# Loading the first units of a grouped normalization in row halves over two DMA queues

## The chip, the cores and the metric

The kernel runs on one core of a Trainium2 chip. The metric is the device time of one execution in microseconds (us), as the median of several runs. A core has five engines: TensorE (PE in the profile), VectorE (DVE), ScalarE (ACT), GpSimd (POOL) and SyncE (SP). The transfers between the chip's memory (HBM) and the on-chip memory (SBUF) are issued from the instruction streams of SyncE and ScalarE here, and 16 DMA engines carry them out.

## The reference

The input is x with the shape (4, 8, 16, 256, 256) and gamma with (8, 16), both in float32. Every one of the 4 x 8 x 16 = 512 channels is normalized over its own 65,536 values and multiplied by its gamma:

```python
mu = x.mean(axis=(3, 4), keepdims=True)
var = ((x - mu) ** 2).mean(axis=(3, 4), keepdims=True)
x_norm = (x - mu) / np.sqrt(var + 1e-5)
out = x_norm * gamma[None, :, :, None, None]
```

So 134.22 MB are read and as much is written, and each value is needed twice: for the sums of its channel and for its own result.

## The kernel before, in words

The work is cut into 32 units of 16 channels. A unit is a tile of 128 partitions with 8,192 values each (4 MiB); eight partitions hold one channel, and one partition's row is 32 KB, contiguous in HBM. Six tiles, `slots` (`xt` in the profile), live in SBUF for the whole kernel; unit `u` uses slot `u % AHEAD`, with `AHEAD = 6`. A unit's result is written into its own slot, in place.

Nothing is reordered by a scheduler: each engine runs its instructions in the order of the program (`manual_schedule`), and waits are put in where data or slots require it. The tool that builds the program also gives each DMA one of eight semaphores in turn, so a DMA waits for the earlier one that used the same semaphore.

For each unit the loop does the following.

- VectorE sums each row (L103) while ScalarE sums the squares of each row (L104); both go to `st`.
- TensorE multiplies `st` with a constant matrix `navg`, which adds up the eight rows of a channel and gives each row the negative mean and the negative mean of squares (L112, into `ps`).
- VectorE forms the negative variance (L113), ScalarE the square root (L117), VectorE the reciprocal and the product with gamma (L121, L123), and then the whole tile is shifted and scaled in place (L126).
- ScalarE issues the store of the tile (L130). SyncE issues the load of unit `u + 6` into the same slot (the helper `load`, L48), once that store has landed.

Before the loop, the first six loads are issued without any wait, through the helper `load`. Units 0, 2, 4 and 5 go to SyncE's queue; gamma (`g_row`, L54) and units 1 and 3 go to ScalarE's. In the profile q1 is SyncE's queue and q10 ScalarE's. All later loads go to SyncE's queue, all stores to ScalarE's, each queue in order. Store 0 therefore stands behind units 1 and 3 in ScalarE's queue.

Of the kernel before, what the change touches and what calls it, by code (L numbers as in the profile page):

```python
# [1 line left out]

# [4 lines left out]

F32 = mybir.dt.float32
U8 = mybir.dt.uint8
ALU = mybir.AluOpType  # L10
ACTF = mybir.ActivationFunctionType
AX = mybir.AxisListType


@with_exitstack
def kernel(
    ctx: ExitStack,
    tc: tile.TileContext,
    x: bass.AP,
    gamma: bass.AP,  # L20
    out: bass.AP,
):
    nc = tc.nc
    B, G, C, H, W = x.shape
    P = nc.NUM_PARTITIONS
    HW = H * W
    n_ch = B * G * C
    S = 8
    K = P // S
    F = HW // S  # L30
    U = n_ch // K
    NG = (G * C) // K
    AHEAD = 6
    assert HW % S == 0 and (G * C) % K == 0

    xv = x.rearrange("b g c h w -> (b g c h w)").rearrange("(u p f) -> u p f", p=P, f=F)
    ov = out.rearrange("b g c h w -> (b g c h w)").rearrange("(u p f) -> u p f", p=P, f=F)
    gv = gamma.rearrange("g c -> (g c)")

    data = ctx.enter_context(tc.tile_pool(name="data", bufs=1))  # L40
    singles = ctx.enter_context(tc.tile_pool(name="singles", bufs=1))
    psum = ctx.enter_context(tc.tile_pool(name="psum", bufs=4, space=bass.MemoryType.PSUM))
    ctx.enter_context(tc.manual_schedule())

    slots = [data.tile([P, F], F32, name=f"xt{i}") for i in range(AHEAD)]

    def load(u, queue):
        queue.dma_start(out=slots[u % AHEAD][:], in_=xv[u])  # L48


    g_row = singles.tile([1, G * C], F32, name="g_row")
    for u in range(AHEAD):
        if u == 1:
            nc.scalar.dma_start(out=g_row[:], in_=gv[None, :])  # L54
        load(u, nc.scalar if u in (1, 3) else nc.sync)


    eps_t = singles.tile([P, 1], F32, name="eps_t")
    nc.gpsimd.memset(eps_t[:], 1e-5)
    one = singles.tile([1, 1], F32, name="one")  # L60
    nc.gpsimd.memset(one[:], 1.0)
    navg = singles.tile([P, K, S], F32, name="navg")
    nc.gpsimd.memset(navg[:], -1.0 / HW)  # L63
    nc.gpsimd.affine_select(  # L64
        out=navg[:], in_=navg[:], pattern=[[-S, K], [0, S]], compare_op=ALU.is_ge,
        fill=0.0, base=0, channel_multiplier=1,
    )
    nc.gpsimd.affine_select(  # L68
        out=navg[:], in_=navg[:], pattern=[[S, K], [0, S]], compare_op=ALU.is_ge,
        fill=0.0, base=S - 1, channel_multiplier=-1,  # L70
    )
    navg_w = navg[:].rearrange("p k s -> p (k s)")
    root_eps = singles.tile([P, 1], F32, name="root_eps")
    nc.scalar.activation(out=root_eps[:], in_=eps_t[:], func=ACTF.Sqrt)  # L74
    g_rep = singles.tile([1, NG, K, S], F32, name="g_rep")
    g_ps = psum.tile([P, NG], F32, name="g_ps", bufs=1)
    g_col = singles.tile([P, NG], F32, name="g_col")

    nc.vector.tensor_copy(  # L79
        out=g_rep[:],  # L80
        in_=g_row[:].rearrange("o (n k) -> o n k", n=NG).unsqueeze(3).to_broadcast([1, NG, K, S]),
    )
    for n in range(NG):
        nc.tensor.matmul(  # L84
            out=g_ps[:, n : n + 1],
            lhsT=g_rep[:, n].rearrange("o k s -> o (k s)"),
            rhs=one[:],
            start=True, stop=True,
        )
    nc.vector.tensor_copy(out=g_col[:], in_=g_ps[:])  # L90

    junk = singles.tile([P, F], U8, name="junk")

    st = singles.tile([P, U, 2], F32, name="st")
    nvar = singles.tile([P, U], F32, name="nvar")
    std = singles.tile([P, U], F32, name="std")
    rstd = singles.tile([P, U], F32, name="rstd")
    scale = singles.tile([P, U], F32, name="scale")

    squares = []  # L100
    for u in range(U):
        t = slots[u % AHEAD]
        nc.vector.reduce_sum(out=st[:, u, 0:1], in_=t[:], axis=AX.X)  # L103
        square = nc.scalar.activation(  # L104
            out=junk[:], in_=t[:], func=ACTF.Square, accum_out=st[:, u, 1:2],
        )
        if u:

            tc.declare_no_dep(square.ins, squares[-1].ins, reason="junk, ordered by the root between")
        squares.append(square)  # L110
        ps = psum.tile([P, 2], F32, name="ps")
        nc.tensor.matmul(out=ps[:], lhsT=navg_w, rhs=st[:, u], start=True, stop=True)  # L112
        nc.vector.tensor_scalar(  # L113
            out=nvar[:, u : u + 1], in0=ps[:, 0:1], scalar1=ps[:, 0:1],
            scalar2=ps[:, 1:2], op0=ALU.mult, op1=ALU.add,
        )
        nc.scalar.activation(  # L117
            out=std[:, u : u + 1], in_=nvar[:, u : u + 1], func=ACTF.Sqrt,
            bias=eps_t[:], scale=-1.0,
        )  # L120
        nc.vector.reciprocal(out=rstd[:, u : u + 1], in_=std[:, u : u + 1])  # L121
        g = u % NG
        nc.vector.tensor_mul(  # L123
            out=scale[:, u : u + 1], in0=rstd[:, u : u + 1], in1=g_col[:, g : g + 1],
        )
        nc.vector.tensor_scalar(  # L126
            out=t[:], in0=t[:], scalar1=ps[:, 0:1], scalar2=scale[:, u : u + 1],
            op0=ALU.add, op1=ALU.mult,
        )
        nc.scalar.dma_start(out=ov[u], in_=t[:])  # L130
        if u + AHEAD < U:
            load(u + AHEAD, nc.sync)


# [1 line left out]
_INS = ['x', 'gamma']  # L136
_OUTS = [((4, 8, 16, 256, 256), 'float32')]


# [23 lines left out]
```

## Time and profile before

| What | Value |
|---|---|
| median of 3 runs | 626.75 us (626.74 to 627.11) |
| the profiled execution's own time | 626.89 us |
| its span in the profile | 625.2 us |
| moved by DMA | 268.46 MB, mean 429 GB/s over the span |
| busy: VectorE, ScalarE, TensorE | 443.2 us, 238.8 us, 21.4 us |
| unit 0: sums begin, store issued | 20.32 us, 35.38 us |

The span runs from the first to the last recorded event of the profiled execution; the 1.7 us between it and the execution's own time lie around it. The profile cuts the span into 40 slices, each 15.6 us long, and gives a digit for each engine and for the DMA engines: 9 means busy for 90% or more. A line of a group names the source line, the engine, the operation, what it writes and reads, how often, the busy time and the mean duration. "To landing" is the time from the issue of a DMA to its completion. A DMA's packet is here one row of 32 KB, moved by one of the 16 DMA engines.

### The profile page before, as it was taken

To read this page: it belongs to the slowest core of one execution; us is meant where nothing else is said; L and a number is where in the kernel's file an instruction comes from. 1 tells how busy PE (TensorE), PEld (TensorE's weight loads), DVE (VectorE), ACT (ScalarE), POOL (GpSimd) and SP (SyncE) were. 2 spreads that over 40 slices of the span, in tenths; PEclk is the share of its full clock that TensorE was granted. 3 is DMA by queue.
4 is the path that set the end of the run, shared out by engine and by line. 5 is a ranking of instruction groups with operands and counts; after the bars stand their busy time and mean duration, and the time that the engine had idled before them with its cause. 6 is when DMAs were issued, how large, how long until landed. Compare 5 with 4: busy or idle time off the path is not lost.

```text
span 625.2 us, 626 instructions
## 1 busy us (share of the span) xinstructions
PE 21.4 (3%) x80; PEld 19.5 (3%) x80; DVE 443.2 (71%) x162; ACT 238.8 (38%) x98; POOL 1.3 (0%) x9
## 2 busy tenths in 40 slices
PE   2000000000000000000000000000000000000000
PEld 2000000000000000000000000000000000000000
DVE  0699999998867668676687766776667867668620
ACT  0444444444444224443244432344423443224400
POOL 0000000000000000000000000000000000000000
DMA  8999999999999999999999999999999999999998
GB/s 369 436 417 424 434 436 436 436 436 437 434 436 434 426 426 430 434 436 436 436 434 434 436 434 434 430 426 430 434 436 436 436 432 434 436 436 434 426 426 365
DMA packets 9220, 268.46 MB, mean 429 GB/s; under 512 B 1025, under 2 KB 1026, under 8 KB 1026
## 3 DMA queue, kind: packets, MB, share of 16 engines
q10 hardware_dynamic: 4898, 142.61, 52.8%
q1 hardware_dynamic: 4320, 125.83, 46.8%
q14 instruction: 2, 0.02, 0.0%
HBM read 134.22 MB, written 134.22 MB: 429 GB/s over the span
## 4 chain that ended last, share of the span: by engine, by line
another core or an unknown queue 64%; DMA 16%; DVE 13%; SPq 1%; PE 1%; issue 0%; ACT 0%
DMA xt<-in_x_dram 9%; DVE st L103 8%; DMA out_dram<-xt 7%; DVE xt L126 4%; SPq L48 1%; PE ps L112 1%; ACT std L117 0%; DVE nvar L113 0%; DVE rstd L121 0%; DVE scale L123 0%
## 5 line engine op out<-in xcount | busy, mean ns | idle before, releaser
L103 DVE TENSOR_REDUCE st<-xt 128x1 f32<-128x8192 f32 x32 | 277.9, 8684 | 111.2 <-DMA xt<-in_x_dram 111.2
L104 ACT ACTIVATE junk<-xt 128x8192 uint8<-128x8192 f32 x32 | 225.0, 7030 | 272.2 <-DMA xt<-in_x_dram 229.0
L126 DVE TENSOR_SCALAR xt<-xt,ps,scale 128x8192 f32<-128x8192 f32 x32 | 145.6, 4550 | 1.2
L117 ACT ACTIVATE std<-nvar,eps_t 128x1 f32<-128x1 f32 x32 | 9.4, 294 | 79.6 <-DVE nvar L113 79.6
L112 PE MATMUL ps<-st,navg 128*128 128x2 f32 x64 | 17.9, 349 | 568.0 <-DVE st L103 568.0
L112 PEld LDWEIGHTS ps<-st,navg 128*128 128x128 f32 x64 | 16.0, 312 | 569.8 <-issue 569.8
L113 DVE TENSOR_SCALAR nvar<-ps 128x1 f32<-128x1 f32 x32 | 9.2, 287 | 23.8 <-PE ps L112 23.8
L121 DVE RECIPROCAL rstd<-std 128x1 f32<-128x1 f32 x32 | 5.3, 164 | 11.6 <-ACT std L117 11.6
L104 ACT ACTIVATION_READ_ACCUMULATOR junk<-xt 128x1 f32 x32 | 6.0, 186 | 0.0
L123 DVE TENSOR_TENSOR scale<-rstd,g_col 128x1 f32<-128x1 f32 x32 | 5.1, 159 | 1.1
L84 PE MATMUL g_ps<-one,g_rep 1*128 1x1 f32 x16 | 3.5, 346 | 2.9 <-DVE g_rep L79 2.9
L84 PEld LDWEIGHTS g_ps<-one,g_rep 1*128 1x128 f32 x16 | 3.5, 325 | 2.9 <-POOL navg L68 2.9
L90 DVE COPY g_col<-g_ps 128x8 f32<-128x8 f32 x1 | 0.2, 166 | 3.7 <-PE g_ps L84 3.7
L74 ACT ACT_TABLE_LOAD x1 | 1.3, 1283 | 2.2 <-issue 2.2
L79 DVE COPY g_rep<-g_row 1x1024 f32<-1x1024 f32 x1 | 0.7, 681 | 2.1 <-DMA g_row<-in_gamma_dram 2.1
L64 POOL TENSOR_SCALAR_AFFINE_SELECT navg<-navg 128x128 f32<-128x128 f32 x1 | 0.4, 403 | 0.1
L68 POOL TENSOR_SCALAR_AFFINE_SELECT navg<-navg 128x128 f32<-128x128 f32 x1 | 0.4, 398 | 0.1
L63 POOL MEMSET navg<- 128x128 f32 x1 | 0.2, 220 | 0.0
L74 ACT ACTIVATE root_eps<-eps_t 128x1 f32<-128x1 f32 x1 | 0.2, 203 | 0.0
L147 POOL MEMSET const-bfloat16-1.0<- 128x1 bf16 x1 | 0.1, 101 | 0.0
L147 POOL MEMSET const-uint8-127<- 128x1 uint8 x1 | 0.1, 101 | 0.0
L147 POOL MEMSET const-float32-0.0<- 128x1 f32 x1 | 0.1, 98 | 0.3 <-issue 0.3
(3 smaller groups left out, 0.3 us busy)
## 6 DMA issues: line engine op xcount, KB each, us to landing
out_dram<-xt ACTq DMA_DIRECT2D x32, 4096.0 KB, 67.1
xt<-in_x_dram SPq DMA_DIRECT2D x30, 4096.0 KB, 33.8
xt<-in_x_dram ACTq DMA_DIRECT2D x2, 4096.0 KB, 33.3
g_row<-in_gamma_dram ACTq DMA_DIRECT2D x1, 0.5 KB
```

What stands on the lines that cost most here:

```text
L48: queue.dma_start(out=slots[u % AHEAD][:], in_=xv[u])
L74: nc.scalar.activation(out=root_eps[:], in_=eps_t[:], func=ACTF.Sqrt)
L79: nc.vector.tensor_copy(out=g_rep[:], in_=g_row[:].rearrange("o (n k) -> o n k", n=NG).unsqueeze(3).to_broadcast([1, NG, K, S]),)
L84: nc.tensor.matmul(out=g_ps[:, n : n + 1], lhsT=g_rep[:, n].rearrange("o k s -> o (k s)"), rhs=one[:], start=True, stop=True,)
L103: nc.vector.reduce_sum(out=st[:, u, 0:1], in_=t[:], axis=AX.X)
L104: square = nc.scalar.activation(out=junk[:], in_=t[:], func=ACTF.Square, accum_out=st[:, u, 1:2],)
L112: nc.tensor.matmul(out=ps[:], lhsT=navg_w, rhs=st[:, u], start=True, stop=True)
L113: nc.vector.tensor_scalar(out=nvar[:, u : u + 1], in0=ps[:, 0:1], scalar1=ps[:, 0:1], scalar2=ps[:, 1:2], op0=ALU.mult, op1=ALU.add,)
L117: nc.scalar.activation(out=std[:, u : u + 1], in_=nvar[:, u : u + 1], func=ACTF.Sqrt, bias=eps_t[:], scale=-1.0,)
L121: nc.vector.reciprocal(out=rstd[:, u : u + 1], in_=std[:, u : u + 1])
L123: nc.vector.tensor_mul(out=scale[:, u : u + 1], in0=rstd[:, u : u + 1], in1=g_col[:, g : g + 1],)
L126: nc.vector.tensor_scalar(out=t[:], in0=t[:], scalar1=ps[:, 0:1], scalar2=scale[:, u : u + 1], op0=ALU.add, op1=ALU.mult,)
```

## The change

Only the first six loads are altered. The helper `load` gets a range of partitions. Units 0 and 2 are each loaded by two DMAs: partitions 0 to 63 from SyncE's queue, partitions 64 to 127 from ScalarE's. Unit 1 stays whole on ScalarE's queue, unit 3 moves to SyncE's. ScalarE's queue now carries gamma, the upper half of unit 0, unit 1 and the upper half of unit 2, and then store 0; SyncE's carries the lower halves of units 0 and 2 and then units 3, 4 and 5. The loop is the same, and its lines stand four lines further down (L103 becomes L107, L130 becomes L134).

```diff
-    def load(u, queue):
-        queue.dma_start(out=slots[u % AHEAD][:], in_=xv[u])
+    def load(u, queue, lo=0, hi=P):
+        queue.dma_start(out=slots[u % AHEAD][lo:hi], in_=xv[u, lo:hi])
 
 
     g_row = singles.tile([1, G * C], F32, name="g_row")
-    for u in range(AHEAD):
-        if u == 1:
-            nc.scalar.dma_start(out=g_row[:], in_=gv[None, :])
-        load(u, nc.scalar if u in (1, 3) else nc.sync)
+    load(0, nc.sync, 0, P // 2)
+    nc.scalar.dma_start(out=g_row[:], in_=gv[None, :])
+    load(0, nc.scalar, P // 2, P)
+    load(2, nc.sync, 0, P // 2)
+    load(1, nc.scalar)
+    load(2, nc.scalar, P // 2, P)
+    for u in range(3, AHEAD):
+        load(u, nc.sync)
```

## The prediction, made before the run

> **What bounds the kernel now.** I read the page first, its slices and queues before its engine rows.
>
> ```profile
> PE 21.4 (3%) x80; PEld 19.5 (3%) x80; DVE 443.2 (71%) x162; ACT 238.8 (38%) x98; POOL 1.3 (0%) x9
> ...
> DMA  8999999999999999999999999999999999999998
> GB/s 369 436 417 424 434 436 436 436 436 437 434 436 434 426 426 430 434 436 436 436 434 434 436 434 434 430 426 430 434 436 436 436 432 434 436 436 434 426 426 365
> DMA packets 9220, 268.46 MB, mean 429 GB/s; under 512 B 1025, under 2 KB 1026, under 8 KB 1026
> ...
> q10 hardware_dynamic: 4898, 142.61, 52.8%
> q1 hardware_dynamic: 4320, 125.83, 46.8%
> ```
>
> No compute engine is full. The DMA row is at 9 in every slice but the first and the last: the 16 DMA engines have work all the time. [...] Then stretches of the span, first the steady middle, then the drain of stores, then the last microseconds:
>
> ```profile
> 60.00:580.00 520.00, 15.62 (x56) 14.04 (x56) 392.03 (x143) 207.91 (x85) 0.00 (x0) 1.00 1.00 434
> 580.00:622.00 42.00, 0.56 (x2) 0.50 (x2) 13.85 (x5) 7.42 (x3) 0.00 (x0) 1.00 1.01 435
> 622.00:625.20 3.20, 0.00 (x0) 0.00 (x0) 0.00 (x0) 0.00 (x0) 0.00 (x0) 1.00 0.07 31
> ```
>
> The last two columns are DMA share and GB/s. 268.46 MB at 434 GB/s is 618.6 us of the 625.2 us; nearly all the rest is the start (nothing moves before 1.8 us) and the tail. The drain, with stores alone in one queue, runs at 435: a single queue fills the engines. So the order of the transfers is worth nothing by itself, and **any time in which the DMA engines move less is added to the end in full**.
>
> The packet records of the trace give the unit. A row of a tile is one 32 KB packet; there are 8,192, so 512 for each engine, and the median one takes 1.213 us (27.0 GB/s). 512 x 1.213 = 621.1 us: back to back from 1.8 us to the drain's end. Each engine's first packet takes about 2.0 us (0.8 extra). The first three packets of each engine are q1's; only then, at 6.13 us, does q10 get its first row, and from there the queues take turns packet by packet.
>
> Last, the waits and the first unit:
>
> ```profile
> SPq L48 <- DMA out_dram<-xt: 536.6, 26, 61.7
> ```
> ```profile
> 20.32 8.69 DVE L103 TENSOR_REDUCE st<-xt 128x1 f32<-128x8192 f32 x1 [13.70 <-DMA xt<-in_x_dram]
> ...
> 35.38 0.35 ACTq L130 DMA_DIRECT2D out_dram<-xt  x1
> ```
>
> From the landing of unit 0 to the issue of store 0 is 35.38 - 20.32 = 15.06 us. SyncE waits for stores, yet its queue never runs dry: a load takes 33.8 us to land by the page's issue rows, against 19.4 us for one tile at half the bandwidth (4.19 MB / 217 GB/s). A store takes 67.1 us, so some three others stand before it. VectorE starting earlier or later is absorbed there.
>
> [...]
>
> **The change part by part.**
>
> *Two more DMA issues.* ScalarE's queue issues three x loads ahead of its table load instead of two, SyncE five in place of four. An issue costs 0.37 to 0.53 us. On ScalarE the table load moves from 2.24 to about 2.7 us, beside a wait for data that ends at 20.32 us: nothing. On SyncE all are issued by about 3 us, with tens of microseconds of data in front: nothing. If that cover were gone, 0.5 us each.
>
> *New waits.* In the changed instruction order, load 5 waits for g_row's semaphore, which it reuses; g_row had landed when g_rep began at 2.06 us, before SyncE gets there. Behind load 5 only load 6 is queued, which waits for store 0. Store 1 waits for the lower half of unit 2; behind it on ScalarE stands the square of unit 2. That half lands before 36 us in any case below, store 1 is ready at 45 or later: nothing. The sums of unit 0 wait for two halves.
>
> *Order and amounts.* ScalarE's queue still carries two units of loads ahead of store 0 (0.5 + 1 + 0.5 for 1 and 3), SyncE's four. So store 0 gets its turn after the same bytes, SyncE has about a unit left when store 0 lands, and neither queue runs dry. If DVE gets unit 0 early, nothing is gained: store 0 stands behind unit 1 and the half of unit 2 anyway.
>
> *The halves.* Each engine now moves 4 x 4 = 16 rows in half tiles (both halves of units 0 and 2). [...] If both of a pair are in the same half together, a packet takes up to 2 x 1.213 us. How exactly do they keep step? The sixteen engines' second packets start between 3.71 and 4.23 us; two taken at random are some 0.2 us apart. [...] So 16 x (1.213 - 0.2) = **+16.2 us**. Ends: d = 0 gives 16 x 1.213 = +19.4; d = 0.52, the whole spread, gives 16 x 0.69 = +11.1. Below nothing isn't excluded by a rule, but only the slow first packets (0.8 us) are there to be won.
>
> The lost time lies wholly on the bound resource, so the sum is 626.89 + 16.2 = 643.1 for the profiled execution; the median stands 0.14 us under it: 643.0.
>
> **The rivals.**
>
> *Pairs out of step.* One engine of a pair is in a lower half while the other is in an upper one; then both go at full rate in units 0 and lower 2. Lost remain the three packets before q10's first row, 3 x 1.0, and the upper half of unit 2, which alternates with whole rows from SyncE's queue: [...] 4 x 1.213 = 4.9. Sum +7.9: 634.7, with its spread 634 to 638. For it: queues alternate halves. Against: all engines start together.
>
> *Not slower: ports don't bind.* The engine's own rate, [...] is the 27.0 GB/s, or the halves go each to engines of their own. Then a half row takes 1.21 us, all packets still follow each other, and the 32 extra completion records cost too little to see: 626.8. It decides when the mean extra of a half row is under 1.25 / 16 = 0.08 us. For it: nothing in this trace shows a slow row after the first. [...]
>
> *Faster through an earlier first unit.* Unit 0 would be the tenth packet of each engine, 1.81 + 0.8 + 10 x 1.213 = 14.7 us, some 5 us early. That would count if VectorE set the end; it has 71% and the stores queue 67 us. Worth at most the 0.8 us: 626.0, inside the 0.2%.
>
> **How the numbers follow.** 0.2% is 1.25 us, about what a measurement of this kernel can tell from no change. In step 0.54, out of step or between 0.21, ports don't bind 0.23, a gain beyond 0.2% 0.02. So slower 0.75, same 0.23, faster 0.02. The likeliest gives 643.0, its own range is 637.9 to 646.2. Both slower cases hold 0.75, so the range has to reach down into the third: 626.6 to 646.5.
>
> **What would show it.** Right: packets of half rows near 2.2 us; the first two slices of GB/s well under 300 (a packet of 2.2 us on 16 engines is 238 GB/s) and another dip near 50 to 60 us, where the upper half of unit 2 alternates with whole rows (two packets in 3.4 us, about 310 GB/s); from then on 434 as before; unit 0's sum starts near 1.81 + 0.8 + 10 x 2.2 = 25 us, later than before, not earlier. Loads still 33.8 us to landing. Wrong: unit 0's sum at 15 us with 430 GB/s in slices 1 to 3 (ports don't bind), or slices after the fifth that fall below 426 (a queue that runs dry, which I excluded).

## The result, and the profile after

The changed kernel takes 647.32 us (median of 4 runs, 647.11 to 647.74) against 626.87 us before in the same comparison: a ratio of 1.0327 (95% interval 1.0309 to 1.0345), or 20.45 us more. The forecast was 643.0 us, slower, with a range up to 646.5: the direction and the place of the loss held, the size lies above the range. The 16.2 us in the forecast rest on an estimate of the author's that no trace of before shows: a half row takes up to twice the measured 1.213 us, less a lag d that stays the same from row to row. Three of the experiments below (e6_lag, e9_middle and e10_contig16) spread by more than 1.5% among their own runs; of those I use single times and stretches of the profile, and no ratio.

The page of the changed kernel, the rows that answer to those shown of before:

```profile
PE 21.4 (3%) x80; PEld 19.5 (3%) x80; DVE 443.4 (69%) x162; ACT 238.8 (37%) x98; POOL 1.3 (0%) x9
...
DMA  9999999999999999999999999999999999999998
GB/s 195 227 420 264 448 426 424 450 424 428 445 424 432 443 424 434 440 424 434 442 422 436 440 422 438 438 422 442 434 422 448 428 422 448 428 426 444 426 432 351
DMA packets 9252, 268.46 MB, mean 416 GB/s; under 512 B 1057, under 2 KB 1058, under 8 KB 1058
...
q10 hardware_dynamic: 4914, 142.61, 52.7%
q1 hardware_dynamic: 4336, 125.83, 46.8%
```

Bytes and the busy time of the engines are the same; 32 small packets more come with the two more DMAs (1,057 under 512 B against 1,025). The DMA row is even fuller than before, at 9 from the first slice on. Busy hides the loss: it is in the row below. Slices 1, 2 and 4 move 195, 227 and 264 GB/s, and from slice 5 on the row looks like that of before. In slices 1 and 2 the DMA engines were occupied and moved half of before's 369 and 436 GB/s.

The same stretches of both kernels show it without the averaging of the slices. The last two columns are DMA share and GB/s. First before, then the changed kernel:

```profile
3.00:26.00 23.00, 3.42 (x16) 3.33 (x16) 5.84 (x2) 6.40 (x3) 0.00 (x0) 1.00 1.00 432
26.00:36.00 10.00, 0.56 (x2) 0.50 (x2) 8.82 (x6) 1.96 (x4) 0.00 (x0) 1.00 0.98 423
36.00:50.00 14.00, 0.56 (x2) 0.50 (x2) 12.82 (x5) 7.19 (x3) 0.00 (x0) 1.00 1.00 412
50.00:65.00 15.00, 0.56 (x2) 0.50 (x2) 13.82 (x6) 7.42 (x3) 0.00 (x0) 1.00 0.99 428
65.00:600.00 535.00, 16.18 (x58) 14.54 (x58) 401.21 (x146) 215.09 (x87) 0.00 (x0) 1.00 1.00 433
```
```profile
3.00:26.00 23.00, 3.42 (x16) 3.33 (x16) 0.17 (x1) 1.49 (x2) 0.00 (x0) 1.00 0.96 207
26.00:36.00 10.00, 0.00 (x0) 0.00 (x0) 7.91 (x1) 7.12 (x2) 0.00 (x0) 1.00 1.01 285
36.00:50.00 14.00, 0.56 (x2) 0.50 (x2) 5.93 (x5) 0.29 (x1) 0.00 (x0) 1.00 1.00 431
50.00:65.00 15.00, 0.56 (x2) 0.50 (x2) 13.60 (x5) 7.42 (x3) 0.00 (x0) 1.00 1.02 275
65.00:600.00 535.00, 16.18 (x58) 14.53 (x58) 401.29 (x146) 215.08 (x87) 0.00 (x0) 1.00 1.00 433
```

Until about 34 us the halves of unit 0 and the lower half of unit 2 are in flight, from 50 to 65 us the upper half of unit 2; between them unit 1 and the whole rows of unit 3 go at full speed. Time lost, as the bytes missing at before's rate: 23 x (432 - 207) / 432 = 11.98, 10 x (423 - 285) / 423 = 3.26 and 15 x (428 - 275) / 428 = 5.36 us, together 20.6 us. Between 36 and 50 us the changed kernel wins back 14 x (431 - 412) / 412 = 0.6 us. That leaves 20.0 of the 20.8 us by which the spans differ (646.0 - 625.2). From 65 to 600 us both run at 433 GB/s: nothing is lost there and nothing won back.

The trace also has a record of each packet, with its start and its duration but without its engine. Following each packet to the one that starts where it ends gives 16 chains of some 512 rows each, one for each DMA engine. What is said below of the rows of an engine is read from these chains.

The first unit and SyncE's waits, the changed kernel:

```profile
28.09 8.69 DVE L107 TENSOR_REDUCE st<-xt 128x1 f32<-128x8192 f32 x1 [21.46 <-DMA xt<-in_x_dram]
...
43.14 0.36 ACTq L134 DMA_DIRECT2D out_dram<-xt  x1
```
```profile
SPq L48 <- DMA out_dram<-xt: 556.0, 26, 80.9
```

Unit 0, split over two queues, begins its sums at 28.09 us; whole, on one queue, it had begun at 20.32. From there to store 0 it takes 15.05 us as before. SyncE's longest wait, load 6 for store 0, grows from 61.7 to 80.9 us, but loads still take 33.8 us to land and stores 67.1, both as before: the queues behind are as full as they were.

### The profile page after: what moved, and what is told of

Same layout as the page of the kernel before. It is cut to its first block, busy times and chain, and to the rows that moved or that the text cites. A ratio compares the mean times of both kernels' runs of the same rounds, so it can differ in the third digit from the quotient of the medians.

```text
span 646.0 us, 633 instructions
## 1 busy us (share of the span) xinstructions
PE 21.4 (3%) x80; PEld 19.5 (3%) x80; DVE 443.4 (69%) x162; ACT 238.8 (37%) x98; POOL 1.3 (0%) x9
## 2 busy tenths in 40 slices
DMA packets 9252, 268.46 MB, mean 416 GB/s; under 512 B 1057, under 2 KB 1058, under 8 KB 1058
## 4 chain that ended last, share of the span: by engine, by line
another core or an unknown queue 65%; DMA 20%; DVE 9%; SPq 1%; PE 0%; issue 0%; ACT 0%; ACTq 0%; DVEq 0%
DMA xt<-in_x_dram 13%; DMA out_dram<-xt 7%; DVE st L107 5%; DVE xt L130 3%; SPq L48 1%; PE ps L116 0%; ACT std L121 0%; DVE nvar L117 0%; DVE rstd L125 0%; DVE scale L127 0%; ACTq L48 0%; ACTq L53 0%; DVEq L107 0%
## 5 line engine op out<-in xcount | busy, mean ns | idle before, releaser
L107 DVE TENSOR_REDUCE st<-xt 128x1 f32<-128x8192 f32 x32 | 277.9, 8685 | 131.8 <-DMA xt<-in_x_dram 131.8
L130 DVE TENSOR_SCALAR xt<-xt,ps,scale 128x8192 f32<-128x8192 f32 x32 | 145.6, 4550 | 1.2
## 6 DMA issues: line engine op xcount, KB each, us to landing
out_dram<-xt ACTq DMA_DIRECT2D x32, 4096.0 KB, 67.1
xt<-in_x_dram SPq DMA_DIRECT2D x29, 4096.0 KB, 33.8
```

The source lines that it names most:

```text
L130: nc.vector.tensor_scalar(out=t[:], in0=t[:], scalar1=ps[:, 0:1], scalar2=scale[:, u : u + 1], op0=ALU.add, op1=ALU.mult,)
```

## The experiments

Three theories went in. **P**: rows that lie together in one half of the partitions hold each other up, so what counts is where the rows of a DMA lie. The "ports" and "pairs" of the recorded texts are the author's guess at what holds them up; the traces show the times of the rows, and neither of these. **Q**: what costs is a unit shared by two queues, or the larger number of DMAs. **S**: 64 rows are a bad shape wherever they lie.

### e1_cols: halves by columns

```diff
-        queue.dma_start(out=slots[u % AHEAD][lo:hi], in_=xv[u, lo:hi])
+        queue.dma_start(out=slots[u % AHEAD][:, lo:hi], in_=xv[u, :, lo:hi])
```

(with F // 2 in place of P // 2)

> Units 0 and 2 are halved by columns (128 rows x 4,096) in place of rows, with the same queues, order, bytes and number of DMAs as the change. Theory P [...]: [...] 626.9 us, within 1 us of before, and the first two slices at 430 GB/s. Rival Q (a unit shared by both queues, or two more DMAs, is what costs): 646 to 648 us as after the change. Rival S (a DMA of 64 rows is slow for its shape): as P.

627.25 us, ratio 1.0001 (0.9993 to 1.001). The first sum, here on L106:

```profile
15.64 8.69 DVE L106 TENSOR_REDUCE st<-xt 128x1 f32<-128x8192 f32 x1 [9.01 <-DMA xt<-in_x_dram]
```

The same queues, order, bytes and number of DMAs cost nothing (ratio 1.0001), so Q falls. Unit 0 is there 4.7 us earlier than before, and the end doesn't move: an early first unit is worth nothing here, as the prediction had it.

### e2_unit0: only unit 0 by row halves

```diff
-    load(2, nc.sync, 0, P // 2)
+    load(2, nc.sync)
     load(1, nc.scalar)
-    load(2, nc.scalar, P // 2, P)
```

> Only unit 0 is split by row halves over both queues; unit 2 is loaded whole from SyncE's queue. 8 half rows per engine in place of 16. P, Q and S alike: about half the loss, +10 us, 637 us, if each half row costs about 1.25 us; a loss that is one event at the start (first use of both queues) would stay at +20 us.

637.08 us, ratio 1.0157 (1.0142 to 1.0172): 9.9 us, half of the loss for half of the rows, 1.24 us for each of 8 half rows of an engine.

```profile
3.00:25.00 22.00, 3.42 (x16) 3.34 (x16) 0.17 (x1) 1.04 (x2) 0.00 (x0) 1.00 0.97 220
25.00:600.00 575.00, 17.29 (x62) 15.54 (x62) 428.86 (x155) 229.92 (x93) 0.00 (x0) 1.00 1.00 433
```

### e3_one_queue: both halves on one queue

```diff
-        load(u, nc.scalar if u in (1, 3) else nc.sync)
+    load(0, nc.sync, 0, P // 2)
+    load(0, nc.sync, P // 2, P)
...
+    load(2, nc.sync, 0, P // 2)
+    load(2, nc.sync, P // 2, P)
```

> The queues of before (units 0, 2, 4, 5 on SyncE's, 1 and 3 on ScalarE's), but units 0 and 2 each as two DMAs of 64 rows one behind the other on SyncE's queue. P: 16 half rows per engine, each beside whole rows of units 1 and 3: [...] +19 to +21 us, 646 to 648 us. Q: no unit is shared by both queues, so under +2 us. S: as P.

654.10 us, ratio 1.041 (1.0376 to 1.0443): 27 us, more than the change itself and more than any theory had said. Q falls again, since no unit is shared here. Now nearly every half row stands beside a whole row of the other queue, until the last half is in at about 69 us:

```profile
3.00:26.00 23.00, 3.44 (x16) 3.35 (x16) 0.17 (x1) 0.71 (x2) 0.00 (x0) 1.00 1.00 256
50.00:65.00 15.00, 0.56 (x2) 0.50 (x2) 13.82 (x6) 7.42 (x3) 0.00 (x0) 1.00 1.02 262
70.00:600.00 530.00, 15.62 (x56) 14.03 (x56) 393.90 (x141) 214.18 (x85) 0.00 (x0) 1.00 1.00 433
```

By the packet records the rows of the lower halves take 2.2 to 2.3 us on average and those of the upper halves 2.55, and the whole rows between them, 1.213 us elsewhere, take 1.75. In an engine's time that is 19 us too much in half rows and 8.7 in whole ones. 27 / 16 = 1.7 us for each half row: it costs itself and its neighbour.

### e4_stride: even and odd partitions

```diff
-        queue.dma_start(out=slots[u % AHEAD][lo:hi], in_=xv[u, lo:hi])
+        queue.dma_start(out=slots[u % AHEAD][lo:P:step], in_=xv[u, lo:P:step])
```

(lo 0 on SyncE's queue, lo 1 on ScalarE's, step 2)

> Units 0 and 2 are split into even and odd partitions (64 rows at a step of 2) in place of lower and upper halves; queues and order as in the change. [...] P, if 16 engines take four consecutive rows each: [...] still about +20 us, 647 us; P, [...] 627 us. S: 647 us. Q: 647 us.

627.55 us, ratio 1.0008 (0.9999 to 1.0016). In the stretches in which the change ran at 207 and 285 GB/s:

```profile
3.00:26.00 23.00, 3.97 (x18) 3.82 (x18) 9.31 (x4) 8.90 (x5) 0.00 (x0) 1.00 0.98 422
26.00:36.00 10.00, 0.00 (x0) 0.00 (x0) 5.60 (x3) 0.89 (x1) 0.00 (x0) 1.00 1.04 449
```

S falls: 64 rows at a step of 2 are as fast as 128 (before has 432 and 423 GB/s here). What counts is where the rows lie. Of P's two cases the 627 us came; how the rows are dealt to the engines was not seen.

### e5_step8, e10_contig16 and e11_cols8: eight DMAs for unit 0

All three load unit 0 by eight DMAs on SyncE's queue, with the queues of before for the rest.

```diff
+    for j in range(8):
+        load(0, nc.sync, j, 8)                               # e5: partitions j, j + 8, ...
+        load(0, nc.sync, 16 * j, 16 * j + 16)                # e10: 16 neighbours
+        load(0, nc.sync, j * F // 8, (j + 1) * F // 8)       # e11: 128 rows, an eighth of the columns
```

> Queues of before; unit 0 comes as eight DMAs of 16 partitions at a step of 8 (0, 8, 16, ... and so on), one behind the other on SyncE's queue. Each DMA is one row for each of 16 engines, eight rows in partitions 0 to 63 and eight in 64 to 127[...]. P [...]: 8 shared rows per engine, about +10 to +14 us, 637 to 641 us. P', a limit of each half of 64 partitions as a whole (half the engines in each half is no overload): 627 to 628 us. Q (more DMAs cost): seven more DMAs, at most what e1 leaves for two, so about 628 us.

> As e5_step8 (eight DMAs of 16 rows for unit 0 on SyncE's queue), but with 16 neighbouring partitions in each DMA. P [...] a row takes about four times as long, 5 us; 8 x 3.7 = +30 us, 657 us. P [...] 10 us a row, +70 us, 697 us. Q (the number of DMAs is what e5_step8 paid for): as e5_step8, 638 us.

> Unit 0 as eight DMAs of 128 rows x 1,024 columns on SyncE's queue: the number of DMAs of e5_step8 [...]. P: 627 to 628 us. Q (the number of DMAs): 638 us as e5_step8.

e5_step8: 638.26 us, ratio 1.0181 (1.0165 to 1.0196), 11.2 us. e10_contig16: 653.86 to 671.11 us; the profiled run is the fastest of these, 26.8 us over before. e11_cols8: 629.43 us, 1.0049 (1.0031 to 1.0068), 2.4 us. The first stretch of each, in this order:

```profile
3.00:26.00 23.00, 3.54 (x16) 3.48 (x16) 0.17 (x1) 0.71 (x2) 0.00 (x0) 1.00 0.95 296
```
```profile
3.00:26.00 23.00, 3.43 (x16) 3.34 (x16) 0.17 (x1) 0.72 (x2) 0.00 (x0) 1.00 0.92 182
```
```profile
3.00:26.00 23.00, 3.54 (x16) 3.48 (x16) 0.38 (x2) 1.49 (x2) 0.00 (x0) 1.00 1.02 433
```

Each of the eight DMAs has 16 rows. The step of 8 puts eight of them into each half of the partitions, as in a whole tile, whose rows take 1.213 us, so a limit of a half as a whole (P') would have been free. So would a limit of each eight neighbouring partitions, since the 16 rows have one in each such group. Yet they take 2.2 us. Those of sixteen neighbours take 3.6 to 4.4 us on average, mostly about 3.75: longer again, but not the 4.9 us (4 x 1.213) of four rows in turn, and far from 10. The loss of 26.8 us comes near the 30 us expected only because the whole rows of units 1 and 3 beside them lose 7 us too, which the expectation had left out. The number of DMAs explains 2.4 us at most of either.

So the limit is narrower than a half, and the rows stand in this order: 1.213 us in whole tiles, 2.2 for 16 at a step of 8, about 3.75 for sixteen neighbours. What holds them up, and why sixteen neighbours take less than four times 1.213 us, stays open.

### e6_lag: eight engines one row behind

```diff
+    load(5, nc.sync, 0, 8)
     load(0, nc.sync, 0, P // 2)
```

> The change, with one DMA of 8 rows (unit 5, rows 0 to 7, loaded again later) ahead of all others on SyncE's queue. Eight engines get one row from it and so stand one packet behind the other eight. [...] the rival of the prediction, pairs out of step, 8 us over before plus the row itself, 634 to 638 us. If the pairs fall back into step, or other engines are paired: 647 to 650 us.

The runs took 672.80 to 702.56 us, at least 46 us over before: neither case. The extra row did its part: in the packet records the rows start in two groups of eight, some 1.3 us apart. Still a half row takes 2.4 us:

```profile
3.00:41.00 38.00, 4.00 (x18) 3.85 (x18) 10.65 (x6) 8.90 (x5) 0.00 (x0) 1.00 0.99 202
...
55.00:76.00 21.00, 0.56 (x2) 0.50 (x2) 13.85 (x5) 7.42 (x3) 0.00 (x0) 1.00 1.00 214
76.00:600.00 524.00, 15.49 (x56) 13.99 (x56) 382.21 (x136) 207.38 (x83) 0.00 (x0) 1.00 1.00 424
```

So the two groups don't get out of each other's way by standing apart. Which engines hold each other up was not seen, nor whether pairs that are really out of step would run free. While halves are in flight 38 x (433 - 202) / 433 + 21 x (433 - 214) / 433 = 31 us are lost, more than in the change. The 424 GB/s after 76 us (433 in the changed kernel) is a loss of 11 us more, at a time when no half is in flight: some of SyncE's whole rows take 1.4 to 2.0 us there. What starts it, this run doesn't show.

### e7_midload and e8_midstore: halves in the steady part

```diff
-            load(u + AHEAD, nc.sync)                         # e7, in the loop
+            if u + AHEAD in (12, 20):
+                load(u + AHEAD, nc.sync, 0, P // 2)
+                load(u + AHEAD, nc.sync, P // 2, P)
+            else:
+                load(u + AHEAD, nc.sync)
```
```diff
-        nc.scalar.dma_start(out=ov[u], in_=t[:])             # e8, in the loop
+        if u in (12, 20):
+            nc.scalar.dma_start(out=ov[u, : P // 2], in_=t[: P // 2])
+            nc.scalar.dma_start(out=ov[u, P // 2 :], in_=t[P // 2 :])
+        else:
+            nc.scalar.dma_start(out=ov[u], in_=t[:])
```

> The first six loads as before; in the loop the loads of units 12 and 20 are each two DMAs of 64 rows, one behind the other on SyncE's queue, beside whole stores on ScalarE's. 16 half rows per engine. P [...] as e3_one_queue, +27 us, 654 us. P with separate ways in and out: only the half rows themselves are doubled, 16 x 1.2 = +19 us, 646 us. If the loss belongs to the start of the program: 627 us.

> All loads as before; the stores of units 12 and 20 are each two DMAs of 64 rows on ScalarE's queue. 16 half rows per engine are read from SBUF. P in both directions: +19 us (646 us), up to +27 us if they hinder the whole loads beside them. [...] If the half stores hold up ScalarE's stream through the semaphores that they reuse, a dip of the DMA share to under 0.9 shows it.

e7_midload: 644.56 us, ratio 1.0281 (1.0259 to 1.0304), 17.5 us. So the cost belongs to the rows and not to the start of the program. The two stretches that hold them:

```profile
190.00:225.00 35.00, 1.15 (x4) 1.00 (x4) 28.23 (x12) 14.84 (x6) 0.00 (x0) 1.00 1.01 347
...
350.00:390.00 40.00, 1.73 (x6) 1.50 (x6) 29.39 (x14) 15.52 (x9) 0.00 (x0) 1.00 1.00 373
```

They miss 35 x (433 - 347) / 433 + 40 x (433 - 373) / 433 = 12.5 us. The rest is spread: 424 GB/s between them (2.4 us) and a lower last slice (300 GB/s against 365, another 2.4 us). That the total lies near the 19 us expected of half rows alone is chance: by the packet records the half rows take about 1.9 us here (unit 12) and 1.8 (unit 20), not 2.4. Beside whole stores a half load costs less than beside whole loads (17.5 against 27 us); neither case expected rows as short as these, and the runs don't show why.

e8_midstore: 639.37 us, ratio 1.018 (1.0144 to 1.0217), 12.3 us, though one of the four runs took 634.76. The stretch of the first split store, then that of the second:

```profile
275.00:305.00 30.00, 1.17 (x4) 1.00 (x4) 16.48 (x10) 13.61 (x6) 0.00 (x0) 1.00 0.99 378
...
430.00:465.00 35.00, 1.18 (x4) 1.00 (x4) 23.97 (x10) 14.83 (x6) 0.00 (x0) 1.00 1.00 406
```

Here only 30 x (433 - 378) / 433 + 35 x (433 - 406) / 433 = 6.0 us are missing; the last slice of this run moves 197 GB/s where before moves 365, about 6 us more, the DMA engines no longer ending together: their last rows end between 626.6 and 636.1 us, where before they end within 0.8 us. Stores pay too, less than loads (12.3 against 17.5 us) and unevenly; why, these runs don't show.

### e9_middle: partitions 32 to 95 in one DMA

```diff
-    load(0, nc.sync, 0, P // 2)
+    load(0, nc.sync, P // 4, 3 * P // 4)
...
-    load(0, nc.scalar, P // 2, P)
-    load(2, nc.sync, 0, P // 2)
+    load(0, nc.scalar, 0, P // 4)
+    load(0, nc.scalar, 3 * P // 4, P)
+    load(2, nc.sync)
...
-    load(2, nc.scalar, P // 2, P)
```

> Only unit 0 is split: SyncE's queue loads partitions 32 to 95 in one DMA of 64 rows, ScalarE's loads 0 to 31 and 96 to 127 in two DMAs of 32; units 1 to 5 are whole. P [...] 4 shared rows per engine instead of 8: about +5 us, 632 us, against 637 us of e2_unit0. P [...] the middle is doubled and the quarters are fourfold, about +20 us, 647 us. S (64 rows are slow): at least +5 us, and then in SyncE's rows and not in ScalarE's.

One run took 632.44 us, the 632 of P's first case; the three others 649.79 to 651.80, near the 647 of its second, so the total alone shows little. The profile is of one of the long ones, and its last stretch shows the tail of e6_lag again:

```profile
3.00:20.00 17.00, 3.42 (x16) 3.33 (x16) 0.17 (x1) 1.16 (x2) 0.00 (x0) 1.00 0.98 268
...
90.00:600.00 510.00, 14.51 (x52) 13.03 (x52) 358.45 (x131) 191.81 (x79) 0.00 (x0) 1.00 1.00 424
```

While unit 0 is loaded, 17 x (433 - 268) / 433 = 6.5 us are lost, against 22 x (433 - 220) / 433 = 10.8 us in e2_unit0, with four rows of quarters for an engine in place of eight of halves. In the packet records the middle's last row, the one with no quarter's row still in flight, takes 1.21 us on all 16 engines, so the middle is not doubled as the second case has it. This also speaks against a cause on the side of HBM: these 64 rows are 2 MiB in one piece there, just as a half's are, and start only 1 MiB further on. Then 510 x 9 / 433 = 10.6 us go in the long steady part, with no half tile left, and about 5 us in the last two slices.

## Why the prediction was right or wrong

- **What bounds the kernel, and that lost DMA time is added to the end in full**: right. 20.6 us are missing in three stretches and 0.6 won back in a fourth, of 20.8 us on the span.
- **Issues, waits, queues that don't run dry**: right in what they cost. ScalarE's table load starts at 3.23 us, not about 2.7, and SyncE issues its fifth load until about 4 us, not 3, but both are covered. Loads and stores have the same time to landing as before, both kernels move 433 GB/s after 65 us, and e1_cols and e4_stride carry the same extra DMAs on the same queues within 0.1%.
- **Half rows of up to 2 x 1.213 us**: right in kind; they take 2.31 to 2.45 us on average, and by e1, e2, e4, e5, e9 and e10 it is where the rows lie that counts. That it comes from engines in pairs was the author's estimate and was not shown. The place was right too: slices under 300 at the start, 275 GB/s at 50 to 65 us, unit 0 late instead of early.
- **The size, 16 x (1.213 - 0.2) = 16.2**: this step failed, in two terms.
  - The first is the 0.2, a lag worked out from the spread of the starts and taken off each of the 16 rows. The half rows of the changed kernel take 2.31 to 2.45 us on average (each of the four halves by itself), 18.8 us over 1.213 for the 16 rows of an engine. About 0.7 us of it is the slow first row that before has as well. So 18.1 us, or 1.13 a row in place of 1.01: 1.9 us more in all. Lags up to 1.2 us were there and spared these rows nothing: the fourth rows of unit 0's lower half start between 11.43 and 12.62 us on the sixteen engines, and every one takes 2.36 or 2.37 us. Of an engine's 16 half rows 11 follow another half row, and these take 2.36 to 2.58 us; only the 4 that follow a whole row vary with the start, from 1.90 to 2.50. So what a lag spares it spares at the first row of a run of half rows, not at each; this fits the records, but was not tested by itself.
  - The second is a term that the likeliest case put at nothing, without a reason: whole rows beside half rows. Those of units 1, 3 and 4 take 2.6 us too long in all, 1.2, 0.5 and 0.9. Before has 0.6 us of slow rows of its own in unit 4, near 44 us, which are gone after the change, so 2.0 us remain. The prediction had this cost in a rival only, with 4.9 us for the upper half of unit 2. e3_one_queue, where nearly all 16 half rows stand so, shows it larger: 8.7 us.
  - Together 16.2 + 1.9 + 2.0 = 20.1 us of the 20.8.
- **The range**: its upper end, 646.5, is the case of no lag at all, 626.75 + 19.4 = 646.2, with 0.3 to spare. The half rows by themselves stayed inside it (+18.1 us). It had no room for the whole rows beside them, and these 2.0 us carried the time out of it.
- **The rivals**: half rows are not free, at 2.31 to 2.45 us against the 1.21 of the second rival; an earlier unit is worth nothing (e1_cols: 4.7 us early, 0.0001 in the ratio); pairs out of step were not seen.

## What to carry to other kernels

If a kernel is bound by DMA, mind where the rows of a piece lie when you split a tile: by columns (ratio 1.0001) or by partitions at a step of 2 (1.0008) the split was free here, by lower and upper halves it cost 20.45 us. The halves moved at half the rate (207 against 432 GB/s) for as long as both queues held halves. A DMA row that reads 9 everywhere doesn't say that the bytes flow; read the GB/s row below it, stretch by stretch. Price the neighbours of slow rows too: here 16 half rows cost 18 us by themselves, and the whole rows beside them 2 us more in the change and 8.7 us in e3_one_queue.

## What the runs showed of the hardware that I had not expected

64 rows at a step of two partitions run at the full 422 to 449 GB/s, though they are 64 rows. Split stores cost 12.3 us where split loads cost 17.5 us in the same steady part, and about half of the stores' loss came at the end of the program. In the changed kernel a half row's time depends on what its engine moved before it: 2.36 to 2.58 us after another half row, 1.90 to 2.50 after a whole row. And in two kernels (e6_lag, e9_middle) the steady part fell from 433 to 424 GB/s long after the last split tile, 11 us that come from slow whole rows on SyncE's queue; what starts it is open.
